# Low parts of the projection weights: made once, kept in DRAM, read back for later tile groups

## The chip, the cores and the metric

The kernel runs on one core of a Trainium2 chip. The metric is the device time of one execution in microseconds (us), lower being better. The core's engines are PE (TensorE), DVE (VectorE), ACT (ScalarE), POOL (GpSimd) and SP (SyncE, which here only issues transfers). ACT and POOL issue transfers as well.

## The reference

The reference is one decoder block on 1024 tokens of width 1024, in float32:

```
h    = RMSNorm(x) * (1 + scale1) + shift1
proj = h @ w_in + b_in                      # 1024 x 2304: q, k, v and the gates of a short convolution
mix  = concat(attention, gated conv) @ w_out + b_out      # 1024 x 1024
x    = x + gate1 * mix
h2   = RMSNorm(x) * (1 + scale2) + shift2
q    = h2 @ w_query                         # 1024 x 2048: 8 heads, two halves each
idx, gates = top 16 pairs of keys per head and token, softmax
out  = sum over the chosen experts of gates * gelu(h2 . peer_u[idx]) * peer_v[idx]
y    = RMSNorm(x + gate2 * out)
```

What the change touches are the three products with w_in, w_out and w_query. Their blocks of 128 columns number 18, 8 and 16, so 42 in all.

## The kernel before, in words

**Tiles and groups.** The 1024 tokens are eight tiles of 128. They go through the front of the block (norms, three projections, attention, convolution, choice of keys) in three groups: tiles 0 to 2, tiles 3 to 5, tiles 6 and 7. Names with `g0`, `g1`, `g2` belong to the three groups. After the front, from about 1035 us on, a dense stage computes all experts for five tiles, while the remaining three tiles gather theirs row by row (`u`, `v`, issued by POOL at line 949). The order of the dense stage is written out by hand. The order within the front is set by a scheduler, which interleaves the emitted instructions on every engine; each engine then runs its own list strictly in order.

**Weights in two parts.** A float32 weight block is split into a high part H, which is the block rounded to the type of PE's operands (fp32r), and a low part L, which is the block minus H. Each projection block (`lin`, line 268) is then three chains of matmuls: H with the high part of the activations, H with their low part, L with their high part. A block is 1024 x 128, handled as two halves of 128 x 512, and takes 24 matmuls for each group. `Weights.load` makes these parts: SP issues the transfer of the raw block (line 218, 512 KB, two buffers), ACT copies each half to H (line 223), POOL subtracts to get L (line 224). H and L have four buffers of half a block each, so two blocks. `take` hands out one block and calls `load` for the next. The list of 42 blocks is run three times, once for each group, so there are 126 loads, 252 H copies and 252 L subtractions.

**What else is in the front.** While groups 1 and 2 run, DVE also chooses the experts of finished tiles (`select`, lines 682 to 729, small and bf16 instructions on `eq`, `e`, `t`, `gates`) and builds, for the dense tiles, a table of gates: DVE makes one-hot rows `oh` (line 823), POOL or ACT multiplies them by the gates (line 836 or 832), PE multiplies them together (`G`, line 846), ACT copies the result to `stg` (line 847) and issues a 2 MB store to `G_d` (line 849), twenty times. `oh` has three buffers, `stg` two. In the query projection, POOL also makes the small tiles `tb` and `cand` for the search for the largest keys, and SP loads the keys (`keyg`, line 620). Line 607 loads a row `bcg` that DVE needs at line 610. In group 0, ACT, DVE and PE also compute the conditioning vectors from `wada` (48 loads of 512 KB).

**Waits of transfers.** Transfers issued by SP and by ACT share eight semaphores in turn. A transfer whose semaphore was last used eight transfers earlier waits until that earlier one has landed.

Of the kernel before, what the change touches and what calls it, by code (L numbers as in the profile page):

```python
# [9 lines left out]
F32 = mybir.dt.float32  # L10
# [5 lines left out]
ALU = mybir.AluOpType  # L16
PSUM = bass.MemoryType.PSUM

P = 128
# [3 lines left out]
NC = D // P  # L23
# [61 lines left out]
def block_kernel(  # L85
# [18 lines left out]
    nc = tc.nc  # L104
    cst = ctx.enter_context(tc.tile_pool(name="cst", bufs=1))
    dr = ctx.enter_context(tc.tile_pool(name="dr", bufs=1, space=bass.MemoryType.DRAM))
# [46 lines left out]
    with ExitStack() as fctx:  # L153
# [48 lines left out]
        class Weights:  # L202


            def __init__(self):
                self.src = [(w_in, k) for k in range(18)] + [(w_out, k) for k in range(NC)]
                self.src += [(w_query, k) for k in range(16)]
                self.src *= len(GROUPS)
                self.at, self.ready = 0, []

            def load(self):
                if self.at == len(self.src):
                    return
                dram, k = self.src[self.at]
                name = f"{self.at}"
                self.at += 1
                raw = fs.tile([P, NC, P], F32, tag="wraw", name=f"raw_{name}", bufs=2)
                nc.sync.dma_start(raw.rearrange("p c j -> p (c j)"), dram[k])
                for q in range(2):
                    src = raw[:, q * (NC // 2) : (q + 1) * (NC // 2), :]  # L220
                    H = fs.tile([P, NC // 2, P], F32R, tag="wH", name=f"H_{name}_{q}", bufs=4)
                    L = fs.tile([P, NC // 2, P], F32R, tag="wL", name=f"L_{name}_{q}", bufs=4)
                    nc.scalar.copy(H, src)  # L223
                    nc.gpsimd.tensor_tensor(L, src, H.bitcast(F32), op=ALU.subtract)  # L224
                    self.ready.append((H, L))

            def take(self):
# [641 lines left out]
        def finish(i, acc):  # L869


            def load(name, src):
                t = row(f"{name}{i}")
                nc.sync.dma_start(t, src)
                return t

            g2 = load("g2", g2_d[0].partition_broadcast(P))
            yield
            yield
            yield  # L880
            nc.vector.tensor_tensor(acc, acc, g2, op=ALU.mult)
            xr = load("xr", x1_d[i])
            yield
            yield
            yield
            nc.vector.tensor_tensor(acc, acc, xr, op=ALU.add)
            fg = load("fg", final_g.partition_broadcast(P))
            yield
            ss = cst.tile([P, 1], F32, tag="ssf", name=f"ssf{i}", bufs=2)
            nc.scalar.activation(xr, acc, AF.Square, accum_out=ss)  # L890
            nc.scalar.activation(ss, ss, AF.Sqrt, scale=1.0 / D, bias=eps)
            yield
            yield
            r = cst.tile([P, 1], F32, tag="rf", name=f"rf{i}", bufs=2)
            nc.vector.reciprocal(r, ss)
            nc.vector.scalar_tensor_tensor(xr, acc, r, fg, op0=ALU.mult, op1=ALU.mult)
            yield
            nc.sync.dma_start(out[i * P : (i + 1) * P, :], xr)
# [499 lines left out]
```

## Time and profile before

| | us |
|---|---|
| median of 3 runs | 2877.15 |
| lowest and highest | 2874.75, 2879.05 |
| the profiled execution | 2879.28 |
| its span in the trace | 2877.2 |

| over the span | busy us | share |
|---|---|---|
| PE | 2667.0 | 93% |
| DVE | 2215.0 | 77% |
| POOL | 1907.3 | 66% |
| ACT | 1034.2 | 36% |

The span is what the trace covers of the profiled execution, which took 2.1 us more. A share over the whole span mixes the front with the dense stage, which is 64% of the time; what a change in the front is worth has to be read in stretches of the front. In the trace, `idle before <- X` behind an instruction says how long its engine stood idle and what ended that. An engine written with a q (SPq, ACTq) is its instruction queue issuing a transfer.

### The profile page before, as it was taken

The page shows a single profiled execution, that of the slowest core. Times are in us where ns is not written, and L with a number is a line of the kernel's source. Part 1 is how long each engine was busy: PE and PEld are TensorE (multiplying, and loading weights), DVE is VectorE, ACT ScalarE, POOL GpSimd, SP SyncE. Part 2 cuts the span into 40 slices and gives each one's busy share as a digit, 9 for nine tenths or more (in the row PEclk, how much of TensorE's full clock was granted, in tenths as well). Part 3 has the DMA queues.
Part 4 walks back from the last instruction along what each step waited for, and adds up shares of the span by engine and source line. Part 5 has one row for each costly group of instructions (what it writes and reads, how often), then busy time and mean ns, then how long its engine had stood idle before and what let it go on. Part 6 is the DMA issues. An engine that isn't in the chain of part 4 may idle for free.

```text
span 2877.2 us, 43985 instructions
## 1 busy us (share of the span) xinstructions
PE 2667.0 (93%) x15358; PEld 2429.5 (84%) x15358; DVE 2215.0 (77%) x4645; ACT 1034.2 (36%) x2219; POOL 1907.3 (66%) x1894
## 2 busy tenths in 40 slices
PE   5998888988799778999999999999999999999997
PEld 4888866888678777999999889999999899999996
DVE  8826996869976877877777777777778777777776
ACT  3445445564466532222222322222222322222222
POOL 2445755657555756777777677777777777777771
PEclk9999898898899999999999999999999999999999
DMA  8635257773456757898988898898988889898884
GB/s 313 216 105 166 89 139 212 227 195 99 108 142 167 208 162 266 312 328 323 344 320 323 304 337 325 322 334 315 337 323 320 323 330 338 311 339 322 318 325 148
DMA packets 381978, 750.61 MB, mean 261 GB/s; under 512 B 188598, under 2 KB 194742, under 8 KB 381756
## 3 DMA queue, kind: packets, MB, share of 16 engines
q0 software_dynamic: 110592, 402.70, 38.0%
q1 hardware_dynamic: 107004, 303.16, 30.5%
q10 hardware_dynamic: 164160, 41.94, 6.8%
q8 instruction: 120, 1.97, 0.3%
q14 instruction: 102, 0.84, 0.1%
HBM read 695.79 MB, written 51.92 MB: 260 GB/s over the span
## 4 chain that ended last, share of the span: by engine, by line
PE 63%; DVE 5%; DMA 1%; ACT 1%; POOL 1%; issue 1%; another core or an unknown queue 0%; SPq 0%; DVEq 0%; ACTq 0%; POOLq 0%
PE A L1122 29%; PE V L1168 28%; PE G L846 2%; DVE oh L823 1%; PE lin_g2in L268 1%; PE lin_g2q L268 1%; DMA xr<-x1d 1%; PE lin_g2o L268 1%; DVE u L970 1%; DVE eq L728 0%; DMA V<-in_peer_v_dram 0%; POOL L L224 0%; DMA Gb<-G_d 0%; DVE eq L724 0%; DVE eq L717 0%
## 5 line engine op out<-in xcount | busy, mean ns | idle before, releaser
L949 POOL DMA_INDIRECT u<-in_peer_u_dram,idx x384 | 365.5, 952 | 235.0 <-DVE u L970 83.4
L224 POOL TENSOR_TENSOR L<-raw,H 128x512 fp32r<-128x512 f32 x252 | 335.4, 1343 | 273.7 <-ACT H L223 176.3
L1168 PE MATMUL V<-VH,WH 128*128 128x512 f32 x1280 | 503.0, 393 | 12.7 <-DVE acc_d L1175 9.6
L949 POOL DMA_INDIRECT v<-in_peer_v_dram,idx x384 | 363.4, 946 | 208.5 <-DVE u L970 67.7
L1168 PE MATMUL V<-VL,WH 128*128 128x512 f32 x1280 | 500.7, 391 | 0.0
L977 DVE SCALAR_TENSOR_TENSOR acc<-v,wv,acc 128x1024 f32<-128x1024 f32 x381 | 489.7, 1285 | 13.1 <-DMA v<-in_peer_v_dram,idx 7.5
L1168 PE MATMUL V<-VH,WL 128*128 128x512 f32 x1280 | 499.7, 390 | 0.0
L1127 ACT ACTIVATE A<-A 128x384 f32<-128x384 f32 (+1 forms) x256 | 107.7, 422 | 990.3 <-PE A L1122 750.9
L970 DVE SCALAR_TENSOR_TENSOR u<-u,h 128x1024 f32<-128x1024 f32 x384 | 457.7, 1214 | 2.8 <-DMA u<-in_peer_u_dram,idx 2.6
L1122 PE MATMUL A<-hDH,UH 128*128 128x384 f32 (+1 forms) x2048 | 344.5, 311 | 20.5 <-ACT UH L1085 19.2
L1105 POOL TENSOR_TENSOR VL<-V,VH 128x512 fp32r<-128x512 f32 x256 | 331.6, 1308 | 34.8 <-ACT VH L1101 32.4
L1122 PE MATMUL A<-hDH,UL 128*128 128x384 f32 (+1 forms) x2048 | 343.3, 310 | 9.8 <-POOL UL L1089 9.8
L1122 PEld LDWEIGHTS A<-hDH,UH 128*128 128x128 f32 x2048 | 321.1, 190 | 31.2 <-ACT UH L1085 20.0
L1139 DVE TENSOR_TENSOR A<-A,Gb 128x384 f32<-128x384 f32 (+1 forms) x256 | 126.4, 498 | 281.2 <-ACT A L1127 214.3
L1122 PE MATMUL A<-hDL,UH 128*128 128x384 f32 (+1 forms) x2048 | 341.3, 309 | 0.0
L1089 POOL TENSOR_TENSOR UL<-U,UH 128x1024 fp32r<-128x1024 f32 x128 | 308.7, 2412 | 33.2 <-ACT UH L1085 31.0
L1122 PEld LDWEIGHTS A<-hDH,UL 128*128 128x128 f32 x2048 | 311.6, 189 | 10.9 <-POOL UL L1089 10.9
L1122 PEld LDWEIGHTS A<-hDL,UH 128*128 128x128 f32 x2048 | 311.0, 189 | 0.0
L1168 PEld LDWEIGHTS V<-VH,WH 128*128 128x128 f32 x1280 | 241.7, 189 | 62.9 <-DVE acc_d L1175 13.8
L1168 PEld LDWEIGHTS V<-VH,WL 128*128 128x128 f32 x1280 | 241.6, 189 | 51.7
L1168 PEld LDWEIGHTS V<-VL,WH 128*128 128x128 f32 x1280 | 241.7, 189 | 45.1
L1175 DVE TENSOR_TENSOR acc_d<-acc_d,V 128x512 f32<-128x512 f32 x310 | 211.9, 684 | 55.0 <-PE V L1168 53.0
(313 smaller groups left out, 4324.0 us busy)
## 6 DMA issues: line engine op xcount, KB each, us to landing
U<-in_peer_uT_dram SPq DMA_DIRECT2D x128, 512.0 KB
V<-in_peer_v_dram SPq DMA_DIRECT2D x256, 256.0 KB
G_d<-stg ACTq DMA_DIRECT2D x20, 2048.0 KB
Gb<-G_d SPq DMA_DIRECT2D x64, 640.0 KB
raw<-in_w_in_dram SPq DMA_DIRECT2D x54, 512.0 KB
wada<-in_w_ada_dram SPq DMA_DIRECT2D x48, 512.0 KB
raw<-in_w_query_dram SPq DMA_DIRECT2D x48, 512.0 KB
raw<-in_w_out_dram SPq DMA_DIRECT2D x24, 512.0 KB
```

Of the source, the lines that this page charges most:

```text
L224: nc.gpsimd.tensor_tensor(L, src, H.bitcast(F32), op=ALU.subtract)
L268: nc.tensor.matmul(ps[:, :w], wt[:, c, :], h[:, q * (NC // 2) + c, o : o + w], start=(k == 0), stop=(k == 3 * NC - 1),)
L949: nc.gpsimd.indirect_dma_start(out=t, out_offset=None, in_=peer_u if which == "u" else peer_v, in_offset=bass.IndirectOffsetOnAxis(ap=idx[ ...
L970: nc.vector.scalar_tensor_tensor(t, t, 1.0, h2[i], op0=ALU.mult, op1=ALU.mult, accum_out=av[i][:, j : j + 1])
L977: nc.vector.scalar_tensor_tensor(acc[i], t, wv[i][:, j : j + 1], acc[i], op0=ALU.mult, op1=ALU.add)
L1089: nc.gpsimd.tensor_tensor(L, Ur.pop(b), Up[b][0].bitcast(F32), op=ALU.subtract)
L1105: nc.gpsimd.tensor_tensor(L, Vr.pop(v), Vp[v][0].bitcast(F32), op=ALU.subtract)
L1122: nc.tensor.matmul(ps[:, : n * P], u[:, c, :], h[:, c, sl], start=(k == 0), stop=(k == 3 * NC - 1))
L1127: nc.scalar.activation(w, w, AF.Gelu)
L1139: nc.vector.tensor_tensor(w3, w3, g, op=ALU.mult)
L1168: nc.tensor.matmul(ps, w[:, ts_], v, start=(n == 0), stop=(n == 3 * CB - 1))
L1175: nc.vector.tensor_tensor(accs[0][:, t, hs], accs[0][:, t, hs], ps, op=ALU.add)
```

## The change

For the first run through the list of 42 blocks, L is made as before, and each half is also stored to a DRAM tensor `low` (84 stores of 256 KB, issued by SP when the next block is loaded). For the second and third run, L is not computed: SP issues a transfer from `low` straight into the buffer of L (168 loads of 256 KB). H is made as before in all three. The 168 subtractions of groups 1 and 2 on POOL are gone.

```
             def __init__(self):
                 self.src = [(w_in, k) for k in range(18)] + [(w_out, k) for k in range(NC)]
                 self.src += [(w_query, k) for k in range(16)]
+                self.n = len(self.src)
                 self.src *= len(GROUPS)
                 self.at, self.ready = 0, []
+
+                self.low = [dr.tile([P, 2, NC // 2, P], F32, name=f"low{k}") for k in range(self.n)]
+                self.keep = []
 
             def load(self):
...
                 name = f"{self.at}"
+                low, first = self.low[self.at % self.n], self.at < self.n
                 self.at += 1
                 raw = fs.tile([P, NC, P], F32, tag="wraw", name=f"raw_{name}", bufs=2)
                 nc.sync.dma_start(raw.rearrange("p c j -> p (c j)"), dram[k])
+                while self.keep:
+                    nc.sync.dma_start(*self.keep.pop(0))
                 for q in range(2):
...
                     nc.scalar.copy(H, src)
-                    nc.gpsimd.tensor_tensor(L, src, H.bitcast(F32), op=ALU.subtract)
+                    if first:
+                        nc.gpsimd.tensor_tensor(L, src, H.bitcast(F32), op=ALU.subtract)
+                        self.keep.append((low[:, q], L.bitcast(F32)))
+                    else:
+                        nc.sync.dma_start(L.bitcast(F32), low[:, q])
                     self.ready.append((H, L))
```

Three places show how the instructions stand. First SP, in the input projection of group 1; the number behind `raw_` or `L_` is the block's place in the list of 126, and 0 or 1 its half. Before:

```order
L218 DMA raw_52_4253<-in_w_in_dram 128x1024
L218 DMA raw_53_4323<-in_w_in_dram 128x1024
L218 DMA raw_54_4404<-in_w_in_dram 128x1024
L218 DMA raw_55_4551<-in_w_in_dram 128x1024
L218 DMA raw_56_4609<-in_w_in_dram 128x1024
```

and with the change:

```order
L235 DMA L_50_0_4168<-low8_174 128x512
L235 DMA L_50_1_4172<-low8_174 128x512
L223 DMA raw_52_4379<-in_w_in_dram 128x1024
L235 DMA L_51_0_4247<-low9_175 128x512
L235 DMA L_51_1_4251<-low9_175 128x512
L223 DMA raw_53_4449<-in_w_in_dram 128x1024
L235 DMA L_52_0_4382<-low10_176 128x512
```

The two loads of a block's L stand just ahead of the raw load of the block two later, whose buffer that block gives back.

Second POOL, in the input projection of group 1, where tile 0's gate table is built (`u2` are gathers of tile 2). Before:

```order
L224 TENSOR_TENSOR L_55_0_4554<-raw_55_4551,H_55_0_4553 128x512
L949 DMA u2_9_4399<-in_peer_u_dram,idx2_3906 128x1024
L224 TENSOR_TENSOR L_55_1_4558<-raw_55_4551,H_55_1_4557 128x512
L836 TENSOR_TENSOR oh_0_92_4379<-oh_0_92_4379,gT0_3671 128x512
L949 DMA u2_10_4459<-in_peer_u_dram,idx2_3906 128x1024
```

and with the change:

```order
L847 TENSOR_TENSOR oh_0_92_4505<-oh_0_92_4505,gT0_3797 128x512
L960 DMA u2_9_4525<-in_peer_u_dram,idx2_4032 128x1024
L847 TENSOR_TENSOR oh_0_96_4566<-oh_0_96_4566,gT0_3797 128x512
L847 TENSOR_TENSOR oh_0_100_4576<-oh_0_100_4576,gT0_3797 128x512
L960 DMA u2_10_4585<-in_peer_u_dram,idx2_4032 128x1024
```

The subtractions that stood between the multiplications of `oh` are gone, and the one for position 92 has moved ahead of a gather.

Third SP, at the start of the query projection of group 2, around the load of `bcg`. Before:

```order
L218 DMA raw_113_9837<-in_w_query_dram 128x1024
L218 DMA raw_114_9906<-in_w_query_dram 128x1024
L607 DMA bcg2_9618<-a2_d_81 128x1024
L608 DMA bcg2_9618<-s2_d_83 128x1024
L620 DMA keyg2_2_9833<-in_keysT_dram 128x128
L218 DMA raw_115_10002<-in_w_query_dram 128x1024
```

and with the change:

```order
L223 DMA raw_114_10032<-in_w_query_dram 128x1024
L235 DMA L_113_0_9966<-low29_195 128x512
L631 DMA keyg2_2_9959<-in_keysT_dram 128x128
L235 DMA L_113_1_9970<-low29_195 128x512
L223 DMA raw_115_10128<-in_w_query_dram 128x1024
L618 DMA bcg2_9744<-a2_d_81 128x1024
L619 DMA bcg2_9744<-s2_d_83 128x1024
```

`bcg` now stands behind the loads of block 113's L and behind raw block 115.

## Rows read from the trace of the kernel before

**Rows 1.** Busy time by stretch: length; PE, PEld, DVE, ACT, POOL; PE clock, DMA share, GB/s
```profile
0.00:50.00 50.00, 16.47 (x80) 14.66 (x80) 38.13 (x66) 16.68 (x27) 9.27 (x30) 1.00 0.94 351
50.00:300.00 250.00, 238.73 (x1303) 213.85 (x1304) 160.94 (x556) 120.69 (x281) 117.74 (x147) 0.95 0.51 166
300.00:450.00 150.00, 119.74 (x660) 109.83 (x659) 144.11 (x463) 71.63 (x171) 93.34 (x130) 0.87 0.45 127
450.00:705.00 255.00, 226.92 (x1330) 207.72 (x1328) 191.44 (x731) 139.69 (x318) 152.78 (x228) 0.91 0.65 189
705.00:800.00 95.00, 69.31 (x444) 62.66 (x444) 91.23 (x180) 41.37 (x102) 55.98 (x55) 0.85 0.41 101
800.00:870.00 70.00, 67.02 (x445) 56.16 (x445) 50.47 (x99) 38.10 (x89) 34.48 (x28) 0.95 0.59 155
870.00:1035.00 165.00, 142.44 (x1119) 137.73 (x1117) 125.92 (x413) 98.74 (x244) 114.56 (x155) 0.94 0.70 186
1035.00:2877.00 1842.00, 1786.33 (x9988) 1626.91 (x9988) 1412.82 (x2146) 507.31 (x989) 1329.15 (x1123) 0.99 0.85 311
```
**Rows 2.** Groups of POOL, 300 to 1045 us: busy, mean ns, idle before
```profile
L224 POOL TENSOR_TENSOR L<-raw,H 128x512 fp32r<-128x512 f32 x170 | 225.0, 1335 | 109.9 <-ACT H L223 83.0 <-PE lin_g1in L268 15.0 <-PE lin_g1q L268 3.3
L836 POOL TENSOR_TENSOR oh<-oh,gT 128x512 f32<-128x512 f32 x120 | 130.2, 1087 | 111.1 <-DVE oh L823 108.7 <-PE pT L414 1.4 <-PE lin_g2o L268 0.3
```
**Rows 3.** Timeline, DVE's selection beside POOL: start us, duration us, engine, line
```profile
332.54 1.19 DVE L682 TENSOR_TENSOR gates<-scv 128x128 f32<-128x128 f32 x1
...
343.59 5.53 POOL L224 TENSOR_TENSOR L<-raw,H 128x512 fp32r<-128x512 f32 x4 [4.39 <-ACT H L223]
...
345.08 1.69 DVE L717 TENSOR_TENSOR eq<-ca,iota 128x1024 bf16<-128x1024 bf16 x1
...
351.78 0.68 DVE L717 TENSOR_TENSOR eq<-cb,iota 128x1024 bf16<-128x1024 bf16 x1
...
751.73 1.28 DVE L705 TENSOR_SCALAR t<-cu 128x128 f32<-128x128 uint32 x1
```
**Rows 4.** Waits, 300 to 1045 us: total us, times, longest
```profile
POOL oh L836 <- DVE oh L823: 108.7, 61, 8.9
...
PE G L846 <- POOL oh L836: 40.8, 31, 5.0
...
PE lin_g2q L268 <- POOL L L224: 5.8, 2, 4.9
```
**Rows 5.** Timeline, POOL ahead of a matmul of G
```profile
441.80 1.27 POOL L224 TENSOR_TENSOR L<-raw,H 128x512 fp32r<-128x512 f32 x1
...
443.02 1.04 POOL L836 TENSOR_TENSOR oh<-oh,gT 128x512 f32<-128x512 f32 x1
...
444.11 2.07 PE L846 MATMUL G<-oh 128*128 128x128 f32 x8 [5.04 <-POOL oh L836]
...
981.63 1.16 PE L846 MATMUL G<-oh 128*128 128x128 f32 x8 [0.91 <-POOL oh L836]
```
**Rows 6.** Timeline of transfers: issue of a raw block, and the copy it ends
```profile
997.96 0.33 SPq L218 DMA_DIRECT2D raw<-in_w_query_dram  x1
...
1001.51 0.62 ACT L223 CAST H<-raw 128x512 fp32r<-128x512 f32 x1 [1.85 <-DMA raw<-in_w_query_dram]
```
**Rows 7.** Chain that ended last: a 256 KB load at the start of the dense stage
```profile
1034.59 6.49 DMA V<-in_peer_v_dram
```
**Rows 8.** Stores of the gate table, group 2: two issues, and a stretch of 2 us
```profile
882.80 0.37 ACTq L849 DMA_DIRECT2D G_d<-stg  x1
...
897.77 0.37 ACTq L849 DMA_DIRECT2D G_d<-stg  x1
...
894.00:896.00 2.00, 2.00 (x18) 1.83 (x17) 1.06 (x2) 0.99 (x2) 0.67 (x1) 1.00 0.43 98
```
**Rows 9.** SP's queue around bcg
```profile
963.89 0.33 SPq L607 DMA_DIRECT2D bcg<-a_d  x1
...
969.29 0.33 SPq L218 DMA_DIRECT2D raw<-in_w_query_dram  x1
```

More of the change, by code (lines that the diff above doesn't have):

```diff
@@ L207, in __init__ @@
                 self.src += [(w_query, k) for k in range(16)]
+                self.n = len(self.src)
                 self.src *= len(GROUPS)
                 self.at, self.ready = 0, []
+                self.low = [dr.tile([P, 2, NC // 2, P], F32, name=f"low{k}") for k in range(self.n)]
+                self.keep = []
             def load(self):
@@ L215, in load @@
                 name = f"{self.at}"
+                low, first = self.low[self.at % self.n], self.at < self.n
                 self.at += 1
@@ L218, in load @@
                 nc.sync.dma_start(raw.rearrange("p c j -> p (c j)"), dram[k])
+                while self.keep:
+                    nc.sync.dma_start(*self.keep.pop(0))
                 for q in range(2):
@@ L223, in load @@
                     nc.scalar.copy(H, src)
-                    nc.gpsimd.tensor_tensor(L, src, H.bitcast(F32), op=ALU.subtract)
+                    if first:
+                        nc.gpsimd.tensor_tensor(L, src, H.bitcast(F32), op=ALU.subtract)
+                        self.keep.append((low[:, q], L.bitcast(F32)))
+                    else:
+                        nc.sync.dma_start(L.bitcast(F32), low[:, q])
                     self.ready.append((H, L))
```

## The prediction

> **What bounds the kernel now.** I read the busy time by stretch first [rows 1], because the shares over the span hide the front. From 1035 us on the dense stage holds 1842 us, with PE busy 97% of it. Its order is written by hand, it contains no L of the projections, and nothing in it changes; it can only begin earlier or later. So the whole effect lies before 1035 us. Group 0 up to 300 us has PE busy 239 of its 250 us after the start: PE bounds it, and it still makes its L on POOL. Groups 1 and 2 are different, and not uniform. From 300 to 450 us DVE is busy 144.1 of 150 us and PE 119.7; from 705 to 800 us DVE is busy 91.2 of 95 and PE 69.3. There DVE sets the pace. In the other three stretches of these groups, PE is busy 436 of 490 us, and no engine is full.
>
> Then I read what POOL does [rows 2]. The subtraction is its largest group, 225.0 us at 1.335 us each. But it is no bottleneck by its load: it and the multiplications of `oh` together are 355 us of 745. So the 225 us cannot come off the end. Three views say what part can.
>
> The first is the timeline of DVE's selection [rows 3]. An `eq` of the same shape takes 0.68 us alone and 1.69 us when a subtraction of POOL runs beside it. Small instructions that take 0.2 to 0.4 us elsewhere take 1.1 to 1.4 us. The two engines stop each other, and it happens where DVE is full.
>
> The second is the table of waits [rows 4]. PE waits 40.8 us for `oh` from POOL, but POOL in turn waits 108.7 us for DVE's `oh`: most of PE's wait is DVE's. PE waits for L itself only 5.8 us, in two pieces.
>
> The third is the timeline before such a wait [rows 5]: at 441.80 us POOL subtracts, at 443.02 it multiplies, and PE has stood idle for 5.04 us. There POOL's queue, not DVE, is late.
>
> **The change part by part.**
>
> *DVE is no longer stopped by the subtraction.* In the two stretches where DVE is full I went through its instructions and took those that overlap mostly with a subtraction and run longer than usual for their form. There are 31, from 332.54 to 751.73 us, of which the first and the last are shown [rows 3]. Duration less usual duration sums to 14.9 us (16 instructions) in the first stretch and 13.2 us (15) in the second, 28.1 us. In a stretch with DVE 96% busy such time is on the path, until PE is next; PE has 30 and 26 us of idle time there. Between nothing and 28 I take 0.6 of it, 17 us, because an instruction that is not stopped by a subtraction may meet another of POOL's, and because the freed time is split over many small handovers.
>
> [...]
>
> *POOL's queue is shorter.* Outside those two stretches, seven of the waits for `oh` have a subtraction directly ahead in POOL's list, from 444.11 to 981.63 us [rows 5]. The part I put down to it is 3.8 us at the first (three subtractions of 1.27) and 9.6 us for the six others, 13.4 us in all. Behind it DVE or ACT is next, so I take half: 7 us. Of the two waits for L, 5.8 us [rows 4], I take 5, as the load will be issued as soon as PE has released the buffer, where POOL came only after its small tiles.
>
> *Gained:* 17 + 7 + 5 = 29 us.
>
> *The loads of L.* 168 transfers, each issued in 0.33 us as a raw load is [rows 6], 55 us on SP, which computes nothing. What can hurt is lateness. An L buffer is released when PE has finished with that half of block k-2, and needed again at the same place of block k less a few matmuls: 44 matmuls later. At the mean of 0.171 us per matmul (226.9 us for 1330) that is 7.5 us from 450 to 705 us, and at 0.127 us (142.4 for 1119) 5.6 us from 870 to 1035 us [rows 1], if PE ran nothing else and never waited. In fact the last stretch holds 24 blocks in 165 us, so 1.83 blocks are 12.6 us. Against that stand two durations: a raw block of twice the size is copied 3.55 us after its issue [rows 6], and a 256 KB load in a crowd of seven took 6.49 us [rows 7]. So the loads mostly arrive in time. I take 3 us for some that don't, and 0 to 38 as the range, the upper end being the second rival.
>
> *SP's order.* What is queued behind a load of L that waits for PE is the raw block two later, which waited for the subtraction of the same half before, and now only for ACT: it comes no later. In the query projection the keys come behind as well, which were behind the raw loads. One transfer does fall back: `bcg` now stands behind block 113's second L and raw block 115. In the trace `bcg` is issued at 963.89 and raw block 115 at 969.29 [rows 9], so it is some 5.4 us later; DVE's instruction that needs it has also been moved down in its list. Price 0 to 5 us; I take 1.
>
> *The stores in group 0.* 84 stores of 256 KB are 22 MB, over 250 us with a DMA share of 0.51 [rows 1]. A store waits for the subtraction for which the raw load behind it waited already, so SP's queue stands no longer than before. The buffer of L is only free once the store has landed; but the store goes out about one block before PE uses that L, so PE releases it later still. Only the start is full (share 0.94 at 351 GB/s in the first 50 us): four stores, 1 MB, are 3 us there. PE's list in group 0 also shifts by a few small matmuls. Price 0 to 10; I take 2.
>
> Costs: 3 + 1 + 2 = 6 us. **Sum:** 29 - 6 = 23 us. The profiled execution took 2879.28 us, 2.1 us above the median. From its span of 2877.2, less 23, plus the 2.1 around it, that is 2856.3; from the median of 2877.15 it is 2854.2. I say **2855**.
>
> **The rivals.**
>
> [...]
>
> *Slower: L comes too late.* In the query projections of groups 1 and 2 (32 blocks), PE does one block after another, and SP's list also holds keys that wait for PE. There are also the stores of the gate table: one issued at 882.80 is done when the transfers fall off near 895 [rows 8], 12 us, and fills all DMA engines meanwhile. If a load then takes longer than the slack of 5.6 to 7.5 us by 1.2 us for each of 32 blocks, it costs 38 us instead of 3: 2854 + 35 = 2889. It decides from about 7 us between issue and landing, or from a gate-table store over the 15.0 us between its issue and the next [rows 8], since `stg` has two buffers. Against it: 3.55 us for twice the bytes at 1000 us.
>
> [...]
>
> *The stops only move.* The multiplications of `oh` (120 of them, 130.2 us in rows 2) stay on POOL, come earlier, and stop DVE instead. In the two full stretches, stops that I put down to other work than the subtraction sum to 12 us already. If the first term falls from 17 to 6 us: 2854 + 11 = 2865.
>
> [...]
>
> **How the numbers follow.** Forecast 0.44, stops move 0.15, more 0.11, nothing shows 0.17, slower 0.13. A measurement of this kernel tells about 0.2% from no change, 5.8 us. The first three lie below 2871.4: 0.70. Nothing shows: same, with 0.01 of it given to slower, as a few us of the costs tip it. So 0.70, 0.16, 0.14. The range reaches from 2838, which leaves out most of "more", to 2882, which takes in "nothing shows" with its costs and leaves out "slower": about 0.2 outside.
>
> **What would show it.** In the changed profile: an `eq` at 0.68 us nearly always in 300 to 450 and 705 to 800 us, and both stretches shorter (they are the first term); PE's wait for `oh` falling from 40.8 towards 25 us; no wait of PE for L from a transfer above a few us in all; group 0 ending within 5 us of where it does; the dense stage at 1842 us. I am wrong if PE waits for L from DRAM for 20 us or more, if the gate-table stores begin to hold up ACT, or if DVE's busy share in those stretches stays while their length stays too.

## The result and the profile after

| | us |
|---|---|
| kernel before, median of 4 runs (lowest, highest) | 2875.95 (2874.37, 2879.05) |
| changed kernel, median of 4 runs (lowest, highest) | 2823.49 (2822.61, 2825.93) |
| ratio, with its 95% interval | 0.9819 (0.9806 to 0.9831) |
| span of the profiled execution, before and after | 2877.2, 2820.8 |

The change takes 52 us off. The forecast was 2855 with a range from 2838 to 2882: the side was right, the gain was more than twice the one forecast, and the time lies below the range.

Where the time went is seen first in when PE starts the matmuls of the three query projections, which close the three groups. The timeline of the matmuls with H gives the times of the first and the last start. Before:

```profile
L268 PE MATMUL lin_g0q<-hDH,H x128: 333/337/669, 226.1 to 309.3; 128*128 128x384 f32 x128
L268 PE MATMUL lin_g1q<-hDH,H x128: 333/336/668, 608.1 to 691.6; 128*128 128x384 f32 x128
L268 PE MATMUL lin_g2q<-hSH,H x128: 278/283/568, 953.1 to 1032.7; 128*128 128x256 f32 x128
```

After:

```profile
L279 PE MATMUL lin_g0q<-hDH,H x128: 333/336/669, 231.5 to 316.5; 128*128 128x384 f32 x128
L279 PE MATMUL lin_g1q<-hDH,H x128: 333/337/669, 576.9 to 660.8; 128*128 128x384 f32 x128
L279 PE MATMUL lin_g2q<-hSH,H x128: 278/283/570, 896.4 to 979.3; 128*128 128x256 f32 x128
```

Group 0 ends 7.2 us later. From there group 1 takes 38.0 us less (344.3 against 382.3) and group 2 another 22.6 us less (318.5 against 341.1). The projections themselves got no shorter (83.9 against 83.5 us for group 1's, 82.9 against 79.6 for group 2's): what got shorter is what lies between them. The dense stage is unchanged: from its first matmul to the end of the span it takes 1840 us before and 1837 after.

Busy time by stretch, after the change (length; PE, PEld, DVE, ACT, POOL; PE's granted clock, DMA share, GB/s), to be held against the same stretches in [rows 1]:

```profile
50.00:300.00 250.00, 236.68 (x1276) 208.33 (x1275) 163.25 (x531) 117.40 (x278) 114.00 (x137) 0.95 0.70 242
300.00:450.00 150.00, 134.01 (x780) 118.50 (x779) 136.04 (x512) 80.56 (x189) 64.76 (x115) 0.94 0.71 215
...
705.00:800.00 95.00, 82.76 (x582) 68.98 (x582) 73.40 (x135) 57.85 (x146) 33.05 (x29) 1.00 0.70 181
```

From 300 to 450 us PE gets through 780 matmuls where it did 660, and its clock is 0.94 instead of 0.87. The DMA share rises everywhere, by the stores in group 0 and by the loads behind it.

The row that the rest of this text uses is that of both groups together: from behind group 0's last query matmul to group 2's last. Before, and then after:

```profile
310.00:1036.00 726.00, 616.06 (x3932) 564.54 (x3930) 594.30 (x1820) 382.23 (x906) 441.35 (x576) 0.90 0.59 162
```

```profile
317.00:983.00 666.00, 587.21 (x3923) 537.72 (x3922) 537.38 (x1804) 382.78 (x908) 229.06 (x399) 0.95 0.81 242
```

These are 60 us less. POOL's busy time falls by 212 us, which is the subtractions. DVE's falls by 57 us, though the program gives DVE nothing less to do: some 3 of the 57 are 16 short instructions that lie outside the row after the change (1820 and 1804), and some 54 are instructions that take less time. PE's falls by 29 us for nearly the same matmuls, and PE's idle time by 31 us (from 109.9 to 78.8).

The waits from 300 to 1045 us, after (engine, who waits for whom: total us, times, longest):

```profile
PE G L857 <- POOL oh L847: 17.4, 19, 2.8
PE lin_g2q L279 <- DMA L<-low: 6.8, 3, 5.7
...
POOL oh L847 <- DVE oh L834: 207.5, 86, 22.9
```

Against [rows 4], PE's wait for `oh` falls from 40.8 to 17.4 us. PE's wait for L only changes its source: 5.8 us from POOL before, 6.8 us from a transfer now. POOL waits for DVE twice as long as it did.

**One stop, followed through.** At 343.59 us before, POOL subtracts four times in 5.53 us [rows 3]. What DVE does meanwhile, in its timeline (start, duration):

```profile
343.72 1.32 DVE L696 TENSOR_SCALAR t<-t 128x128 uint32<-128x128 uint32 x1
...
345.08 1.69 DVE L717 TENSOR_TENSOR eq<-ca,iota 128x1024 bf16<-128x1024 bf16 x1
346.69 1.28 DVE L698 TENSOR_SCALAR fa<-t 128x128 f32<-128x128 uint32 x1
347.90 1.36 DVE L688 TENSOR_TENSOR gates<-gates,gs 128x128 f32<-128x128 f32 x1
...
351.51 0.22 DVE L729 TENSOR_TENSOR e<-eq 128x64 f32<-128x64 bf16 x1
```

After the change these forms take 0.31, 0.73, 0.29 and 0.28 us on average: 4.0 us lost in four instructions. DVE is busy without a gap from there to the `e` at 351.51 us, for which PE's next transpose `eT` waits. PE's timeline at the same place:

```profile
351.87 0.45 PE L810 MATMUL eT<-ident,e 128*128 128x128 f32 x1 [4.87 <-DVE t L695]
...
354.35 1.48 PE L268 MATMUL lin_g1in<-hDH,H 128*128 128x384 f32 x4
...
358.59 0.85 PE L268 MATMUL lin_g1in<-hDL,H 128*128 128x384 f32 x4
```

And the stretches of 2 us there:

```profile
354.00:356.00 2.00, 2.00 (x8) 2.00 (x8) 1.88 (x4) 0.00 (x0) 1.31 (x1) 0.50 0.00 0
...
358.00:360.00 2.00, 2.00 (x14) 2.00 (x13) 1.90 (x4) 1.05 (x2) 1.30 (x1) 1.00 0.00 0
```

PE waits 4.87 us for DVE (the view names `t`, the instruction that ended just behind `e`). When it goes on it is granted half of its clock (0.50), four matmuls take 1.48 us where they take 0.85 a little later, and only at 358 us is the clock at 1.00 again. So the 4 us that DVE lost made most of a pause of PE, and some 3 us of slow matmuls followed. Summed over the stretches of 2 us in groups 1 and 2, PE's busy time multiplied by what its clock is short of 1.00 is 55.2 us before and 26.3 after: 28.9 us, as much as PE's busy time falls.

### The profile page after: what moved, and what is told of

It reads as the page before. It is cut to its first block, busy times and chain, and to the rows that moved or that the text cites. A ratio compares the mean times of both kernels' runs of the same rounds, so it can differ in the third digit from the quotient of the medians.

```text
span 2820.8 us, 44152 instructions
## 1 busy us (share of the span) xinstructions
PE 2642.3 (94%) x15358; PEld 2405.9 (85%) x15358; DVE 2165.8 (77%) x4645; ACT 1033.5 (37%) x2219; POOL 1696.2 (60%) x1726
## 4 chain that ended last, share of the span: by engine, by line
PE 72%; DVE 13%; DMA 5%; issue 4%; ACT 3%; POOL 2%; SPq 0%; ACTq 0%; DVEq 0%; POOLq 0%
PE A L1133 29%; PE V L1179 29%; PE G L857 3%; PE lin_g1in L279 2%; DVE oh L834 2%; DVE adaacc L756 2%; DMA G_d<-stg 1%; PE lin_g0o L279 1%; DMA wada<-in_w_ada_dram 1%; PE lin_g2in L279 1%; PE po L430 1%; DVE Skg L143 1%; DVE ti L145 1%; PE lin_g2o L279 1%; DVE ti L142 1%
## 5 line engine op out<-in xcount | busy, mean ns | idle before, releaser
L847 POOL TENSOR_TENSOR oh<-oh,gT 128x512 f32<-128x512 f32 x120 | 131.3, 1095 | 261.8 <-DVE oh L834 207.5
## 6 DMA issues: line engine op xcount, KB each, us to landing
G_d<-stg ACTq DMA_DIRECT2D x20, 2048.0 KB, 16.7
```

The costliest lines, as they stand in the source:

```text
L847: nc.gpsimd.tensor_tensor(og, og, gT[:, t0 : t0 + 4].unsqueeze(2).to_broadcast([P, 4, NK]), op=ALU.mult)
```

## Experiments

For each kernel the table gives the ratio to the kernel before on the same chip and the same row as above, from behind group 0's last query matmul to group 2's last one, in its profiled execution (us). The profiled execution is one of those behind the ratio and can lie some us off their median; stretches of single profiles also came out 11 and 8 us shorter where nothing was relieved (in stores only, and in group 2 of group 1 only).

| kernel | ratio (95% interval) | length | PE busy | DVE busy | POOL busy | clock |
|---|---|---|---|---|---|---|
| before | 1 | 726 | 616 | 594 | 441 | 0.90 |
| the change | 0.9819 (0.9806, 0.9831) | 666 | 587 | 537 | 229 | 0.95 |
| stores only | 0.9989 (0.9980, 0.9999) | 715 | 609 | 592 | 440 | 0.91 |
| relief only | 0.9798 (0.9782, 0.9815) | 667 | 597 | 539 | 229 | 0.93 |
| load and subtract | 1.0124 (1.0100, 1.0147) | 755 | 628 | 596 | 439 | 0.88 |
| group 1 only | 0.9894 (0.9877, 0.9910) | 687 | 597 | 559 | 337 | 0.94 |
| full stretches only | 0.9885 (0.9869, 0.9902) | 678 | 596 | 553 | 374 | 0.93 |
| the other blocks only | 0.9984 (0.9973, 0.9995) | 710 | 607 | 576 | 294 | 0.91 |
| memset in place | 0.9926 (0.9906, 0.9946) | 694 | 603 | 548 | 434 | 0.92 |
| the change, PE dose | 0.9906 (0.9884, 0.9928) | 697 | 627 | 542 | 232 | 0.94 |
| before, PE dose | 1.0078 (1.0060, 1.0096) | 746 | 653 | 594 | 442 | 0.91 |
| the change, DVE dose | 0.9941 (0.9924, 0.9957) | 707 | 615 | 579 | 225 | 0.91 |
| before, DVE dose | 1.0131 (1.0114, 1.0148) | 760 | 624 | 636 | 440 | 0.89 |

### Stores, loads and POOL's relief apart

**Stores only.**

```
                     nc.gpsimd.tensor_tensor(L, src, H.bitcast(F32), op=ALU.subtract)
                     if first:
                         self.keep.append((low[:, q], L.bitcast(F32)))
```

> Group 0 stores L as in the change, but groups 1 and 2 go on subtracting on POOL; nothing reads the stored L. In the changed kernel the last matmul of group 0's query projection starts 7.2 us later than before (316.5 against 309.3). Theory A, that the 84 stores make those 7 us and that POOL's relief alone makes the gain: 2876 + 7, so 2880 to 2886, group 0 ending near 316, groups 1 and 2 as long as before. Rival, that the 7 us are the scheduler's other order in group 0 or chance, and the stores cost nothing: 2874 to 2878, group 0 ending near 309.

Measured: 2877.2 against 2879.9 on the same chip. Group 0 does end at 317.3 us as in the change, so the 8 us come from the stores or the order that goes with them. But groups 1 and 2 are 11 us shorter in this profile and the dense stage begins at 1034.2 instead of 1037.1 us. Theory A was wrong on the total: here a later end of group 0 cost nothing. Why groups 1 and 2 made up for it is not shown.

This run also bears on a rival that no expectation names, that the gain comes from the other order in which the scheduler lays out the lists. By operation, tile and shape, DVE's instructions of the row before and after the change have 1400 of 1819 in the same order; those of before and of stores only have 1491, hardly more, and the time is the same within 0.2%. So another order is not by itself worth the gain, though some us of the gain may be due to it.

**Relief only.** In groups 1 and 2 the product with L is computed with H in its place; group 0 stores nothing.

```
...
-                        self.keep.append((low[:, q], L.bitcast(F32)))
                     else:
-                        nc.sync.dma_start(L.bitcast(F32), low[:, q])
+                        L = H
```

> No stores and no loads of L: groups 1 and 2 use H in the place of L, so that the product with the low part is computed with the wrong operand (same matmuls, same count). POOL is relieved as in the change, no DMA is added. Theory A (POOL's relief is the whole gain, the DMA only costs: 7 us in group 0 and about 7 us of waits for L): 2823 - 14 = 2809, between 2805 and 2816. Rival B (the gain comes from L arriving by DMA, early and independent of POOL's and ACT's order): 2850 or above. Rival C (stores and loads are hidden): 2821 to 2826.

Measured: 2822.4, 0.9798, where the change gives 0.9819. B is refuted: without a single load the gain is there. Theory A's range is missed, the time lies in theory C's. The stores and loads together cost 0.0021 of the time, 6 us, and the two intervals overlap, so 0 to 12 us. In the two profiles the dense stage begins at 975.3 us here and at 983.9 in the change.

**Load and subtract.** Everything as in the change, and the subtraction too, into a scratch tile.

```
                         nc.sync.dma_start(L.bitcast(F32), low[:, q])
+                        D = fs.tile([P, NC // 2, P], F32R, tag="wD", name=f"D_{name}_{q}", bufs=1)
+                        nc.gpsimd.tensor_tensor(D, src, H.bitcast(F32), op=ALU.subtract)
```

> Stores and loads of L as in the change, but POOL also subtracts as before, into a scratch tile that nobody reads. Theory A: DVE is stopped and POOL's queue is as long as before, and the stores cost their 7 us: 2876 + 7 + 0 to 5 = 2880 to 2890; PE's busy time in groups 1 and 2 near the 625 us of before, its clock near 0.90, PE's wait for oh near 40 us. Rival B (loads make the gain): 2823 to 2835, clock near 0.95.

Measured: 2917.5, 36 us slower than before, and slower than theory A had it. B is dead once more. DVE's busy time is that of before (596 us), and PE waits 39.6 us for `oh`. Theory A had left out that a raw block's transfer now stands on SP behind loads of L that wait for PE, and waits for POOL's subtraction on top: SP waits 111.8 us for it, and PE 17.6 us for H, against 1.3 us before. That this makes the 36 us is argued from these waits, not shown by a run.

**Group 1 only.**

```
-                low, first = self.low[self.at % self.n], self.at < self.n
+                low, first = self.low[self.at % self.n], self.at < self.n or self.at >= 2 * self.n
...
-                        self.keep.append((low[:, q], L.bitcast(F32)))
+                        if self.at <= self.n:
+                            self.keep.append((low[:, q], L.bitcast(F32)))
```

> Group 0 stores L, group 1 reads it back, group 2 subtracts on POOL as before. From the end of group 0's query projection to the end of group 1's the change takes 344.3 us against 382.3 of before, so 38 us; from there to the end of group 2's 318.5 against 341.1, so 22.6 us. Theory A, with gains that add up group by group: 2876 + 7 - 38 = 2845, between 2840 and 2852, group 2 as long as before (341 us). Rival, that group 2's subtractions find the time elsewhere once group 1 has run ahead (or that the gain of group 1 is given back): below 2830 or above 2862.

Measured: 2850.5, inside the expected range. From query projection to query projection as above, group 1 takes 350.5 us where it took 382.3, and group 2 takes 333.5 where it took 341.1; group 0 ends 12.5 us later. Group 1's gain is not given back. Group 2 was expected to be as long as before and is 7.6 us shorter, though nothing was relieved in it.

### Where the subtractions stood

**Full stretches only**, and **the other blocks only**: L is read back for blocks 42 to 55 and 84 to 95, or for all but those (the condition without its `not`). As in group 1 only, stores are issued in group 0 alone.

```
-                low, first = self.low[self.at % self.n], self.at < self.n
+                low, first = self.low[self.at % self.n], self.at < self.n or not (42 <= self.at < 56 or 84 <= self.at < 96)
```

> L is read back only for the blocks whose subtractions stood in the two stretches where DVE was full (group 1's blocks 42 to 55 and group 2's 84 to 95: 52 of 168 subtractions gone); the other 116 are computed as before. Theory D (the gain sits where DVE is full): more than half of it, 2876 - 30 to 2876 - 45, so 2831 to 2846. Rival Q (each subtraction that goes is worth the same, wherever it stands): 52 of 168, 0.31 of 54 us, 2856 to 2863.

> The complement: L is read back for the 116 halves outside the two full stretches and computed on POOL inside them. Theory D: less than half of the gain, 2876 - 10 to 2876 - 24, so 2852 to 2866. Rival Q: 0.69 of 54 us, 2837 to 2842.

Measured: 2843.4 (33 us less) and 2872.0 (some 5 us less). The stretch of both groups in the one and then in the other:

```profile
322.00:1000.00 678.00, 595.81 (x3927) 544.75 (x3925) 552.62 (x1803) 383.04 (x910) 374.10 (x517) 0.93 0.68 194
```

```profile
320.00:1030.00 710.00, 606.98 (x3924) 556.56 (x3922) 576.04 (x1804) 383.87 (x910) 293.61 (x454) 0.91 0.71 209
```

Q is refuted: 52 subtractions give 33 us and 116 give 5. What the time follows is DVE's busy time, not POOL's. Held against stores only (591.8 us), whose row has as few instructions of DVE as theirs, the 52 take 39.2 us off DVE (0.75 us each) and the 116 take off 15.8 us (0.14 each). Together these are 55 us, where the change has 54.4 against the same run. The times don't add up, 33 and 5 against 52 us, and theory D's bound for the second kernel was missed. Group 0 ends at 322.1 and 319.5 us here, so its delay would count twice in the sum; but in stores only the same delay cost nothing, so the gap stays open.

### DVE's stops or POOL's list

**Memset, first try.** A memset of a scratch tile for each subtraction.

```
+                        D = fs.tile([P, NC // 2, P], F32R, tag="wD", name=f"D_{name}_{q}", bufs=1)
+                        nc.gpsimd.memset(D.bitcast(F32), 0.0)
```

> The change, with one memset of a scratch tile of the size of L on POOL for each of the 168 subtractions that went: POOL's list is as long in instructions as before, but these read nothing and wait for nobody. Theory D (what POOL's subtractions cost is that they stop DVE's instructions): an eq of 128x1024 takes 0.68 us also beside a memset, and the time stays within 10 us of the change, 2822 to 2835. Theory Q (what they cost is their time in POOL's list ahead of the multiplications of oh): by the time that a memset takes; at 1.3 us each, 2845 to 2880, PE's wait for oh back near 40 us. If an eq is stretched beside a memset too, the two can't be told apart by this run.

This run did not ask what it should. The scratch depends on nothing, and all 168 memsets ran between 2.5 and 153.4 us, 0.525 us each. 2827.8 us (0.9825) only says that 88 us more on POOL in group 0 hardly matter.

**Memset in place.** Written over the half of the raw block from which ACT has made H, so that the memset stands and waits where the subtraction did, and holds the raw buffer as long.

```
                         nc.sync.dma_start(L.bitcast(F32), low[:, q])
+                        for w in (4, 4, 2):
+                            nc.gpsimd.memset(src[:, :w, :], 0.0)
```

> The change, with three memsets on POOL (two of 128x512, one of 128x256; 1.3 us together by the 0.525 us that a memset of 128x512 took in the run before) on the half of the raw block, once ACT has made H of it, in the 168 places where the subtractions stood. POOL's list is as long as with the subtractions, waits for ACT and holds the raw buffer as they did, but reads nothing. Theory D (the subtraction costs because DVE's instructions are stopped beside it, and a memset does not stop them): DVE's busy time in groups 1 and 2 stays near the 537 us of the change, and the time near it, 2823 to 2836. Theory Q (POOL's list is what costs): 2855 to 2917, the upper end being the run with loads and subtractions. If the memsets stop DVE as the subtractions do, DVE's busy time is near 594 us and the run says nothing.

Measured: 2852.2 (0.9926). POOL's groups (busy, mean ns) show that it is as busy as with the subtractions, 223 us here and 225.0 in [rows 2]:

```profile
L237 POOL MEMSET raw<- 128x512 f32 x333 | 171.2, 533 | 111.0 <-ACT H L230 108.3
L237 POOL MEMSET raw<- 128x256 f32 x168 | 51.8, 320 | 2.5
```

DVE's groups in this kernel:

```profile
L741 DVE TENSOR_TENSOR eq<-eq 128x512 bf16<-128x512 bf16 x24 | 10.2, 427 | 0.2
L730 DVE TENSOR_TENSOR eq<-ca,iota 128x1024 bf16<-128x1024 bf16 x12 | 8.8, 730 | 0.1
L718 DVE TENSOR_SCALAR t<-cu 128x128 f32<-128x128 uint32 x6 | 3.4, 567 | 0.0
```

The same groups before:

```profile
L728 DVE TENSOR_TENSOR eq<-eq 128x512 bf16<-128x512 bf16 x24 | 14.1, 588 | 0.1
L717 DVE TENSOR_TENSOR eq<-ca,iota 128x1024 bf16<-128x1024 bf16 x12 | 13.4, 1118 | 0.1
...
L705 DVE TENSOR_SCALAR t<-cu 128x128 f32<-128x128 uint32 x6 | 3.5, 588 | 0.0
```

And after the change:

```profile
L739 DVE TENSOR_TENSOR eq<-eq 128x512 bf16<-128x512 bf16 x24 | 10.0, 418 | 0.2
L728 DVE TENSOR_TENSOR eq<-ca,iota 128x1024 bf16<-128x1024 bf16 x12 | 8.8, 732 | 0.1
...
L716 DVE TENSOR_SCALAR t<-cu 128x128 f32<-128x128 uint32 x6 | 1.7, 282 | 0.0
L709 DVE TENSOR_SCALAR fa<-t 128x128 f32<-128x128 uint32 x6 | 1.8, 292 | 0.0
```

An `eq` of 128x1024 with two inputs takes 730 ns in the kernel with memsets, 732 without them, and 1118 in the one with subtractions. The instructions that do lie beside POOL's show it: 13 `eq` of 128x512 overlap a memset by over 0.2 us and take 0.44 us on average, 3 overlap a subtraction before and take 1.29. A TENSOR_SCALAR is stopped by either: `t` takes 567 ns with memsets and 588 with subtractions, against 282 after the change. DVE's `oh`, of whose two inputs `keyno` lies in PSUM, is stopped by neither: 1217 ns before, 1217 with memsets and 1215 after, and at most 1.23 us for the 40 of before that overlap a subtraction by over 0.2 us. So DVE's largest group in the row, 191.5 us, was not what the subtractions stopped. Why these forms differ is not shown.

Held against load and subtract, which has the same loads, the same list on POOL and the same hold on the raw buffer, DVE's busy time is 48 us less and the stretch 61 us shorter (694 against 755), 43 of it in group 1 and 19 in group 2. As POOL's instruction no longer reads, and little else differs, that difference is put down to DVE's stops with what PE loses behind them: PE's busy time is 25 us less as well (603 against 628). The scheduler's order differs too. Group 1 shows it best: it takes 348.1 us, 4 us more than in the change and 34 less than before, though POOL is as busy as before. Group 2 is 25 us longer than in the change, as long as before, and so the time lies between the bounds of theory D and theory Q. PE waits 9.6 us for H in the last projection there, and SP 58.5 us for the memset in group 2 before it may load a raw block; so it looks like the held raw buffer rather than POOL's list. A third raw buffer, which would tell, wasn't tried.

### What PE's and DVE's time is worth

**PE dose.** The first matmul of each of the 84 blocks of groups 1 and 2 is done four times.

```
+                                for again in range(3 if k == 0 and self.key != "g0" else 0, -1, -1):
                                     nc.tensor.matmul(
                                         ps[:, :w], wt[:, c, :], h[:, q * (NC // 2) + c, o : o + w],
-                                        start=(k == 0), stop=(k == 3 * NC - 1),
+                                        start=(k == 0), stop=(again > 0 or k == 3 * NC - 1),
                                     )
```

> The change, with the first matmul of each of the 84 projection blocks of groups 1 and 2 done four times (the result is that of the last): 252 more matmuls, 0.17 us each in group 1 and 0.114 in group 2, 36 us of PE at full clock, spread evenly. If PE's time is on the path in these groups (so that the 29 us by which PE's busy time fell were time gained): 2823 + 30 to 2823 + 40. If DVE sets the pace and PE only follows (so that PE's clock is an accompaniment): 2823 to 2835.

> The same 252 matmuls added to the kernel before. If DVE set the pace there in 300 to 450 and 705 to 800 us, less of them shows than in the changed kernel: 2876 + 10 to 2876 + 25. If PE's time counts in full there too: 2876 + 30 to 2876 + 40.

**DVE dose.** A 128x128 piece of each of the 160 `oh` is made twice.

```
+                    nc.vector.tensor_tensor(
+                        oh[:, 0, 0],
+                        keyno,
+                        eT[:, 0, t0 : t0 + 1].to_broadcast([P, NK]),
+                        op=ALU.is_equal,
+                    )
```

> The change, with a quarter of the first half of each of the 160 oh (128x128, overwritten at once by the whole oh) made once more by DVE: 160 instructions of an estimated 0.2 us, a sixth to an eighth of the 1.2 us that 1024 elements take, so some 30 us more of DVE's time, spread over groups 1 and 2. If the time follows DVE's (theory D, by which 57 us of DVE's time are worth the 53 us of the change): 2823 + 25 to 2823 + 38. If DVE's time is mostly covered by PE, and PE's clock made the gain: 2823 to 2836.

> The same 160 instructions in the kernel before. Theory D: 2876 + 25 to 2876 + 38, and more of it than of the same dose on PE (21 of 36 us). If PE sets the pace there: 2876 to 2888.

Some 36 us more on PE cost 0.0087 of the time in the changed kernel (25 us) and 0.0078 in the one before (22 us): two thirds of it. The first lies between its two expected ranges, the second in the one for a DVE that sets the pace. The dose on DVE came out larger than estimated:

```profile
L834 DVE TENSOR_TENSOR oh<-keyno,eT 128x128 f32<-128x128 f32 x160 | 45.0, 281 | 41.0 <-PE G L863 36.9 <-ACT eT L824 2.3 <-POOL oh L853 1.2
```

These 45 us cost 0.0122 in the changed kernel (35 us) and 0.0131 in the one before (38 us): eight tenths of it. Both times lie in theory D's ranges, which were made for a dose of 30 us.

With the DVE dose on the changed kernel PE was given no more to do, yet its busy time in the row went from 587 to 615 us and its clock from 0.95 to 0.91. So the 29 us that PE's busy time fell by the change are no second gain beside DVE's: with a later DVE PE stood idle for 92 us of the row instead of 79 and ran at the lower clock, and this is part of the eight tenths. Nor is the whole fall needed: relief only has the whole gain with PE's busy time 19 us lower (616 to 597).

### Two tries at more

**Filling pauses.** Matmuls that nobody uses, in three pauses of PE: 15 and 8 before the transposes of the second norm of groups 1 and 2, and 40 before group 2's first matmuls with `hSL`.

```
+                fill = bank("t", f"fill{key}")
+                for k in range(0 if key == "g0" else 15 if n == 3 else 8):
+                    nc.tensor.transpose(fill[:, :P], x1[:, k % n, 7 * P : 8 * P], ident)
...
+            fill = bank("t", "fillg2s")
+            for k in range(40):
+                nc.tensor.matmul(fill[:, : 2 * P], last.hH[:, 3, :P], last.hH[:, 3, :], start=True, stop=True)
```

> The change, plus matmuls that compute nothing that is used, put where PE stands idle anyway: 15 of 128x128 before the transposes of group 1's second norm (a pause of 5.31 us at 573.81 in the changed kernel's trace), 8 before those of group 2 (3.29 us at 894.73) and 40 of 128x256 before group 2's first matmuls with hSL (7.47 us at 674.83). Behind each of these pauses the granted clock is at half for some 6 us. Theory C (the clock falls because PE stood idle, and this costs some 3 us behind each pause): no half clock behind the three places, 6 to 10 us less than the change, so 2814 to 2819 where the change gives 2823. Rival (the low clock is not due to the pauses, or it costs nothing on the path): half clock still there, 2823 or, with some of the added matmuls in the way, up to 2828.

Measured: 2836.6 (0.9866, 0.9849 to 0.9882), slower than the change and outside both expected ranges. The profiled execution is the fastest of its four, 2826.7. At the first pause, in stretches of 2 us, after the change and then with the matmuls added:

```profile
572.00:574.00 2.00, 0.19 (x1) 0.19 (x2) 0.93 (x2) 1.75 (x4) 0.00 (x0) 0.50 1.06 408
574.00:576.00 2.00, 1.99 (x9) 1.59 (x8) 0.00 (x0) 1.19 (x2) 0.00 (x0) 0.50 1.07 403
```

```profile
572.00:574.00 2.00, 0.47 (x4) 0.47 (x5) 0.93 (x2) 1.76 (x3) 0.00 (x0) 1.00 1.06 409
574.00:576.00 2.00, 1.29 (x9) 0.82 (x8) 0.36 (x1) 1.58 (x3) 0.00 (x0) 0.82 1.07 402
```

The fall of the clock comes later here (1.00 and 0.82, where the change has 0.50 twice), but it comes, with 0.50 from 576 to 578 us: the 15 matmuls took 1.9 us and left 2.5 us of pause. Nothing is gained by it: group 1's query projection ends at 661.2 us against 660.8, with DVE busy 95.6 of the 100 us from 600 to 700 in the change. The third place was no better. Theory C's time was missed; why the whole is 13 us slower was not looked into further.

**More multiplications on ACT.**

```
-                    if q % 3 == 2:
+                    if q % 2 == 1:
```

> The change, with every second multiplication of oh on ACT instead of every third or fourth (80 of 160 on ACT, 80 on POOL; 120 on POOL before). If POOL's multiplications stop DVE as the subtractions did, DVE's busy time falls and the time with it: 2812 to 2821. If ACT, with some 50 us more, becomes late for H, osg and qqsg: 2825 to 2840.

Measured: 2828.9 (0.9846, 0.9825 to 0.9866), no better than the change. POOL has 44 us less to do, DVE's busy time falls by 4 us only (533.7), and ACT's rises by 45. So a multiplication on POOL costs DVE far less than a subtraction did, 4 us for 40 of them against 54 for 168. No kernel tried here beats the change.

## Why the prediction was wrong

- **What bounds.** Right: group 0 and the dense stage didn't get shorter, and most of the gain lies in the two stretches where DVE was full (33 of 52 us for a third of the subtractions).
- **DVE's stops, 17 us.** This is the step that failed: right mechanism, a third of the size. The count of 28.1 us took only instructions that overlap mostly with a subtraction, in two stretches. By busy time DVE lost some 54 us: 39 in the full stretches and 16 elsewhere, which the prediction put at nothing because no engine was full there. Within the full stretches, each instruction of DVE less the mean of its form after the change sums to 39.7 us in the trace of before, so the sum by form would have held what the count left out. The second error was the factor of 0.6, reasoned and not read. The doses say 0.8, so 54 us are worth an estimated 43 of the 58 that relief only takes off. How the other 15 divide over POOL's list, the waits for L and what PE loses is not shown.
- **PE's clock, left to a rival.** The factor of 0.6 thought of freed time as lost in handovers. But a handover that DVE missed could cost PE slow matmuls too, as the stop at 343.59 us shows in the trace of before: 4.87 us of pause and some 3 us behind it. The author's estimate for the rival "more", 2829, had the clock with 8 us; PE's busy time fell by 29, and by 19 in relief only. It was the nearest, and still short, since it kept the count of 28.1.
- **POOL's queue, 7 us.** Not settled. In group 1 a list as long as before costs 4 us; in group 2 up to 25, with the held raw buffer in it. PE's wait for `oh` did fall by 23 us, more than forecast. In memset in place, with the list kept and DVE not stopped, it is 24.2 us, between the 40.8 before and the 17.4 after: so most of the fall comes from DVE, and some 7 us of it can be the list's.
- **PE's wait for L, 5 us.** Not gained. The largest wait is now 5.69 us:

```profile
972.84 1.22 PE L279 MATMUL lin_g2q<-hSH,L 128*128 128x256 f32 x4 [5.69 <-DMA L<-low]
```

The chain that ended last shows what was under way then:

```profile
953.08 15.28 DMA G_d<-stg
...
968.42 0.33 SPq L223
...
968.85 3.95 DMA L<-low
```

And the page's list of transfers (KB each, median us from issue to landing) has, after:

```profile
L<-low SPq DMA_DIRECT2D x168, 256.0 KB, 4.0
G_d<-stg ACTq DMA_DIRECT2D x20, 2048.0 KB, 16.7
```

The load for which PE waited landed after 3.95 us, like the median of them. It was issued late. SP's next transfer, a raw block, was the eighth behind the gate-table store of 953.08 and so waited for its landing at 968.36; it was issued at 968.42, and the load of L stood behind that raw block. So the rival "slower", the upper end of the 0 to 38 us for late loads, named the right store, but not the way: the store holds SP's queue, and once for long, not in 32 blocks. From 300 to 1045 us SP waits 54.3 us (8 times) for such stores with raw blocks and loads of L, and with neither of them before the change. The prediction has no price for this.

One such store took 12 us before [rows 8], and the median is 16.7 us after. That the loads beside the stores make them longer is not shown by these two figures, as the 12 us are one store, read from where the transfers fall off.

- **Costs, 6 us.** Right in sum: relief only is 0 to 12 us faster than the change. The 2 us for group 0 were too few in its own time (7.2 us), but with the subtractions kept the same delay cost nothing in the total.
- **The rivals on the other side.** "Nothing shows", a time as before with a chance of 0.17, and "the stops only move" fell: `oh` is not stopped (1217 and 1215 ns), but DVE lost time on the path in its other instructions, some 54 us, and the 120 multiplications that stay on POOL stop it little (4 us for 40 of them). "L comes too late" fell as said.

## What to carry to other kernels

When one engine stretches another's instructions (an `eq` from 732 to 1118 ns here), sum the busy time of the stretched one by form against its undisturbed duration, over every stretch and short instructions too: this gives 54 us, 39 of them where picking out clear cases gave 28. Then weigh it by a dose (the same work made a little longer), not by a guess; and where PE follows that engine, a missed handover can cost its pause and slow matmuls behind it (4.87 us and some 3 us here). An engine's own time may be worth little: 212 us less on POOL counted mostly through what POOL did to DVE. And new transfers join the queue of those that are there: look which long transfer their queue may have to wait for (a store of 15.28 us here).

## What was not expected of the hardware

- A memset on POOL leaves DVE's `eq` instructions alone (730 and 427 ns, against 732 and 418 after the change) where subtractions of equal total time stretch them to 1118 and 588, and it stops a TENSOR_SCALAR (567 against 282 ns). DVE's `oh`, one of whose two inputs lies in PSUM, is not stopped by the subtraction either (1217 and 1215 ns). A memset of 128x512 float32 takes 0.53 us there, the subtraction 1.34.
- Behind a pause of PE of 4.87 us its clock was at 0.50 for some 6 us, and with 15 matmuls added in a pause of 5.31 us it fell later (1.00 from 572 to 574 us, where it had been 0.50), without saving time.
- A load of 256 KB that took 3.95 us came 5.69 us late for PE, because SP's queue had to wait for the landing of a store of 15.28 us that ACT had issued eight transfers earlier.
